# Branch B's first three blocks summed together with K outermost, one gate moved into the mLSTM's last head, and four waits given other orders

## The chip, the core and the metric

The kernel runs on one core of a Trainium2 chip. The metric is device time in microseconds, the median of several runs. A core has five engines that run beside each other: TensorE (PE in the profile: matmuls and transposes; PEld is its loading of weights), VectorE (DVE), ScalarE (ACT), GpSimd (POOL) and SyncE (SP), which here only issues DMAs. SPq and ACTq in a timeline are the DMAs that SP and ScalarE issue. TensorE writes its results into PSUM, eight banks of 128 x 512 fp32.

## The reference

One block of a hybrid layer on x of 1024 positions x 1024 channels, all in fp32. What matters of it:

```
h    = rmsnorm(x, norm_g)
proj = h @ w_in                    # a_q a_k a_v a_o a_z a_g  b_q b_k b_v b_z  g_a g_b
y_a  = rmsnorm(mlstm(conv(a_q), conv(a_k), a_v, forward and backward)) * sigmoid(a_o) * silu(a_z)
y_b  = rmsnorm(diff_attention(rope(b_q), rope(b_k), b_v)) * silu(b_z)
mix  = sigmoid(g_a + gb0) * (y_a @ w_branch_a) + sigmoid(g_b + gb1) * (y_b @ w_branch_b)
out  = rmsnorm(x + mix @ w_out, final_g)
```

The mLSTM has 4 heads of 256, the differential attention 8 heads of 128. The "gates" below are g_a and g_b: 16 blocks of 128 channels.

## The kernel before, in words

**Matmuls.** Every fp32 operand is split in a high and a low part (H, L) that TensorE takes at its fast fp32 rate, and each product is three matmuls: H·H, H·L, L·H. The high part is a cast on ScalarE, the low part a subtraction on VectorE or GpSimd. A projection block (`proj`, L556) is 128 output channels in two halves of 512 positions; a half is 24 matmuls (eight k, three each) into one bank "pj", cut into eight pieces of three matmuls (`PIECES`). There are two pj banks.

**Weights.** `load_w` (L196) loads a block's raw weights by DMA, casts them to wH on ScalarE (L225) and subtracts on GpSimd to wL (L230, or L228 in eight steps while the mLSTM runs). There are three wH/wL pairs and two raw tiles. `run` (L527) walks the list of units, prepares weights up to two blocks ahead where a pair is free, and asks for the raw tile of the one behind.

**Order.** The work is a list of units, each some instructions of TensorE with what follows them on other engines. TensorE executes them in the list's order; the orders of the other engines are made by the framework's scheduler. `Weaver.add` appends units as they come. `Weaver.weave` (L110) merges two lists: it keeps a planned clock from the units' costs, and puts next the unit that can start first, by planned delays (`LAG`) and by how long a bank stays taken (`hold`). If one list is at its end, what is left of the other stands alone.

**Stages.** After the opening and the projections of the mLSTM (to about 510 us) come:

1. Attention, eight heads of eight cycles (`da_cycle`, L1166). Cycle t has S(t), the scores; T, eight transposes of the cycle before's probabilities into the two T banks, which are emptied by the cast pH on ScalarE (L1107) and the subtraction pL on VectorE (L1108); in even cycles PV, 48 matmuls; in odd cycles M, two transposes of the result `att` into a T bank with squares on ScalarE. M(3) of a head falls in cycle 1 of the next one and starts a chain of small operations on GpSimd (L1135 to L1138) that gives rb_y. G(0) and G(1), four transposes of rb_y each, follow in cycles 2 and 4, and after each VectorE writes half of y_b and SP stores it. Each head's cycles (`main`) are woven with the next head's q and k projections, rope included, and the like (`nxt`).
2. The mLSTM (`ml_units`, L1391): per head and t, T transposes the weights W, I multiplies with the states, P is W·v, S the next scores; weigh and state update the states from kw. W is made on GpSimd, ScalarE and VectorE from the gate rows gb, k and v. Two `share` numbers per t say how many gate pieces stand ahead of I and behind S. Nine of the gates lie here; the last head's outputs O and its hm scaling come behind them ("late").
3. Two more gates, 32 pieces: 5 ahead of `late`, 3 behind, 24 woven with eight loads of y_b (`load_y`, L1461: DMA to yraw, four tiles; cast on ScalarE, L1465; subtraction on VectorE, L1466). A gate's end (L976) is a tanh on ScalarE into one tile gt and a store that SP issues (L979).
4. Branch B (`mix_units`, L1473): eight blocks, each half summing all eight y_b in one pj bank before the next half starts; then branch A and the output.

## Time and profile before

| | us |
|---|---|
| median of 3 runs | 1687.43 (1687.06 to 1691.82) |
| the profiled execution | 1685.78 |
| its span, first to last instruction | 1684.0 |
| TensorE busy | 1637.8 |
| VectorE / ScalarE / GpSimd busy | 1023.6 / 766.7 / 669.0 |
| mean granted TensorE clock | 0.993 |

How to read the views. The list of waits has one line for each waiting group and its releaser: us in total, times, the longest. A timeline row is start, duration, engine, line of the kernel, operation, tile written <- tiles read, count, and in brackets the idle time of the engine ahead of it and what ended it. A row of the windows is a stretch, its length, then for PE, PEld, DVE, ACT and POOL the busy time with the count of instructions, then the granted clock of TensorE, the busy share of the DMA engines and GB/s. Matmuls overlap in their pipeline: one is about 0.4 us long, but the next starts about 0.23 us after it.

### The profile page before, as it was taken

How to read it: one execution, taken by the hardware profiler on the slowest of the kernel's cores; microseconds unless marked ns; L12 is line 12 of the kernel's file. 1: busy time of each engine (PE TensorE's matmuls, PEld its weight loads, DVE VectorE, ACT ScalarE, POOL GpSimd, SP SyncE). 2: the span in 40 equal slices, each digit the busy share in tenths (PEclk: the TensorE clock that was granted, in tenths of full speed). 3: DMA queues.
4: the chain of work that ended last, by engine and by line, in shares of the span. 5: the costliest groups of instructions: out<-in, count | busy, mean ns of one | idle time of the engine just before them, and what ended most of it. 6: DMA issues, size and time to landing. Idle time of an engine off the chain costs nothing. (4 is left out here: it accounts for less than half of the span.)

```text
span 1684.0 us, 25335 instructions
## 1 busy us (share of the span) xinstructions
PE 1637.8 (97%) x9335; PEld 1375.7 (82%) x9335; DVE 1023.6 (61%) x1817; ACT 766.7 (46%) x1548; POOL 669.0 (40%) x713
## 2 busy tenths in 40 slices
PE   7999999999999999999999999999999998999998
PEld 6898778878778778888878878888988877888886
DVE  5633787686755776777677686614576764145533
ACT  7433555555434444544454445524566744132221
POOL 5744676766652552624445252132222221222000
PEclk9999999999999999999999999999999999999999
DMA  5434444444442312213132221139876427453222
GB/s 184 146 121 132 124 131 138 123 129 123 126 150 63 88 51 68 72 38 89 45 83 56 63 70 48 54 106 295 258 214 199 145 95 256 149 164 99 75 100 76
DMA packets 189711, 199.76 MB, mean 119 GB/s; under 512 B 11930, under 2 KB 143347, under 8 KB 189587
## 3 DMA queue, kind: packets, MB, share of 16 engines
q1 hardware_dynamic: 188386, 196.03, 38.4%
q10 hardware_dynamic: 1200, 2.11, 0.3%
q8 instruction: 74, 1.21, 0.3%
q14 instruction: 51, 0.41, 0.1%
HBM read 124.60 MB, written 56.72 MB: 108 GB/s over the span
## 5 line engine op out<-in xcount | busy, mean ns | idle before, releaser
L570 PE MATMUL pj<-hH,wH 128*128 128x512 f32 x640 | 261.9, 409 | 1.5 <-ACT f L683 1.5
L570 PE MATMUL pj<-hH,wL 128*128 128x512 f32 x640 | 252.5, 395 | 1.3 <-POOL wL L228 1.3
L570 PE MATMUL pj<-hL,wH 128*128 128x512 f32 x640 | 251.6, 393 | 0.0
L1086 DVE TENSOR_REDUCE nm<-S 128x1 f32<-128x1024 f32 x128 | 150.7, 1219 | 110.7 <-PE S L1083 110.7
L230 POOL TENSOR_TENSOR wL<-raw,wH 128x1024 fp32r<-128x1024 f32 x34 | 85.3, 2509 | 186.5 <-ACT wH L225 184.1
L1107 ACT CAST pH<-T 128x512 fp32r<-128x512 f32 x128 | 68.8, 589 | 169.9 <-PE T L150 169.9
L1088 ACT ACTIVATE e<-S,nm 128x1024 f32<-128x1024 f32 x128 | 142.6, 1129 | 7.4 <-DVE nm L1086 7.4
L570 PEld LDWEIGHTS pj<-hH,wL 128*128 128x128 f32 x640 | 121.0, 189 | 29.5 <-POOL wL L228 3.1
L570 PEld LDWEIGHTS pj<-hH,wH 128*128 128x128 f32 x640 | 121.7, 190 | 20.8 <-ACT f L683 1.8
L570 PEld LDWEIGHTS pj<-hL,wH 128*128 128x128 f32 x640 | 121.2, 189 | 19.5 <-DVE hL L721 0.3
L570 PE MATMUL pj<-sl_yb,wH 128*128 128x512 f32 x384 | 121.2, 396 | 4.5 <-DVE sl_yb L1466 2.9
L1083 PE MATMUL S<-kst,qq 64*128 64x512 f32 x768 | 106.1, 408 | 0.0
L1094 DVE SCALAR_TENSOR_TENSOR e<-e,r,e 128x1024 f32<-128x1024 f32 x64 | 101.5, 1587 | 1.8
L225 ACT CAST wH<-raw 128x1024 fp32r<-128x1024 f32 x48 | 50.6, 1055 | 106.5 <-PE pj L570 85.4
L1083 PEld LDWEIGHTS S<-kst,qq 64*128 64x128 f32 x768 | 67.4, 184 | 29.8 <-issue 9.7
L570 PEld LDWEIGHTS pj<-sl_yb,wH 128*128 128x128 f32 x384 | 73.3, 191 | 21.6 <-DVE sl_yb L1466 3.8
L367 PE MATMUL T<-TH,wH 128*128 128x512 f32 x256 | 87.0, 399 | 1.8 <-ACT u L374 1.8
L367 PE MATMUL T<-TH,wL 128*128 128x512 f32 x256 | 86.1, 397 | 1.1 <-ACT u L374 1.1
L514 DVE SCALAR_TENSOR_TENSOR pj<-cin,cols,pj 128x512 f32<-128x512 f32 x128 | 87.0, 749 | 0.0
L1108 DVE TENSOR_TENSOR pL<-T,pH 128x512 fp32r<-128x512 f32 x128 | 82.0, 682 | 5.9 <-ACT pH L1107 5.9
L215 POOL TENSOR_TENSOR wL<-raw,wH 128x512 fp32r<-128x512 f32 x32 | 51.1, 1609 | 67.7 <-ACT wH L214 62.5
L570 PE MATMUL pj<-sl_yb,wL 128*128 128x512 f32 x192 | 75.7, 394 | 0.0
(398 smaller groups left out, 4425.2 us busy)
## 6 DMA issues: line engine op xcount, KB each, us to landing
raw<-in_w_in_dram SPq DMA_DIRECT2D x84, 512.0 KB, 4.0
kst<-hl SPq DMA_DIRECT2D x64, 128.0 KB, 2.4
qq<-hl SPq DMA_DIRECT2D x64, 128.0 KB, 2.4
x<-in_x_dram SPq DMA_DIRECT2D x8, 512.0 KB, 6.2
avH<-tz SPq DMA_DIRECT2D x16, 256.0 KB, 2.0
cak<-y SPq DMA_DIRECT2D x16, 256.0 KB, 2.8
cakH<-cin SPq DMA_DIRECT2D x16, 256.0 KB, 4.8
cakL<-tz SPq DMA_DIRECT2D x16, 256.0 KB, 4.7
```

The costliest lines, as they stand in the source:

```text
L215: self.p.tensor_tensor(out=vw(wL), in0=src, in1=vw(wHf), op=ALU.subtract)
L225: self.a.copy(wH, raw)
L230: self.p.tensor_tensor(out=wL, in0=raw, in1=wHf, op=ALU.subtract)
L367: self.t.matmul(ps, lhsT=l[:, k, :], rhs=r[:, k, :], start=(first and k == 0 and m == 0), stop=(k == 3 and m == 2), skip_group_check=not f ...
L514: v.scalar_tensor_tensor(out=acc, in0=raw[:, o + x:o + x + 512], scalar=w(x), in1=acc, op0=ALU.mult, op1=ALU.add)
L570: self.t.matmul(ps, lhsT=l[:, k, :], rhs=r, start=(n == 0), stop=(n == 23))
L1083: self.t.matmul(ps[:, o], lhsT=qq[r, x, c], rhs=k[r, y, o], start=(m == 0), stop=(m == 2))
L1086: v.tensor_reduce(out=nm, in_=ps, axis=AX.X, op=ALU.max, negate=True)
L1088: a.activation(out=e, in_=ps, func=AF.Exp, bias=nm[:, 0:1], accum_out=Z[:, j, t:t + 1])
L1094: v.scalar_tensor_tensor(out=e0, in0=e, scalar=r[:, 0:1], in1=e0, op0=ALU.mult, op1=ALU.add)
L1107: a.copy(pH[:, :, s], ps)
L1108: v.tensor_tensor(out=pL[:, :, s], in0=ps, in1=pH[:, :, s].bitcast(F32), op=ALU.subtract)
```

## The change

- Branch B: a new `first_units` computes blocks 0, 1 and 2 together. Six banks (a new pool of T banks in the place of the mLSTM's) hold their two halves each; the outer loop runs over k, so that y_b k is used by all of them before y_b k+1. Block 2 runs two steps behind the others. `mix_units` does blocks 3 to 7 as before.
- Gates: ten instead of nine lie in the mLSTM, in the last head's shares and behind it; 16 pieces are left: 5 ahead of `late`, 3 behind, 4 after the first four loads of y_b and 4 after the others. From there on a gate's stores are issued by ScalarE instead of SP (`late`).
- Attention: G goes from cycles 2 and 4 to 3 and 5. The last unit of each head's list, M(2), becomes the first of the next head's.
- mLSTM: the load of gb for chunk 0 of the first head goes from behind the first loads of k and v to right behind the first of them; eight DMAs that stood ahead of it (a v is two) now stand behind it.

```
+GROUP = 3
...
-            (self.a if self.opening else self.q).dma_start(out=self.tg[seg][i][...], in_=t)
+            (self.a if self.opening or self.late else self.q).dma_start(out=self.tg[seg][i][...], in_=t)
...
-        if prev and t in (2, 4):
-            un.append(prev["G"](t // 2 - 1))
+        if prev and t in (3, 5):
+            un.append(prev["G"]((t - 3) // 2))
...
-        un += x["k"](3) + x["v"](3) + x["k"](2) + x["v"](2) + x["k"](1) + x["v"](1) + hl(x, 0)
+        un += x["k"](3) + x["gb"](0) + x["v"](3) + x["k"](2) + x["v"](2) + x["k"](1) + x["v"](1) + x["HL"](0)
...
-                other, share = gates, ((2, 2), (1, 1), (2, 1), (2, 1), (2, 1), (2, 1), (2, 0), (1, 0))
+                other, share = gates, ((2, 2), (2, 2), (2, 2), (2, 2), (2, 2), (2, 1), (2, 1), (2, 1))
...
+    def first_units(self, st):
+        box = {}
+        def piece(i, half, k):
+            if k == 0:
+                box[i, half] = self.bank("T")
+            ps, (wH, wL), (yH, yL) = box[i, half], self.wt[("w_branch_b", 128 * i)], st["gb", k]
+            c = slice(half * 512, (half + 1) * 512)
+            for m, (l, r) in enumerate(((wH, yH), (wH, yL), (wL, yH))):
+                self.t.matmul(ps, lhsT=l[:, k, :], rhs=r[:, c], start=(k == 0 and m == 0), stop=(k == 7 and m == 2))
+            if k == 7:
...
+                self.v.scalar_tensor_tensor(out=m, in0=box["tg", i][:, c], scalar=1.0, in1=ps, op0=ALU.add, op1=ALU.mult)
+        def gates():
+            for i in range(GROUP):
...
+                self.q.dma_start(out=box["tg", i], in_=self.tg["gb"][i])
+        un = [Unit(0.0, gates)]
+        for step in range(8 + 2):
+            for i in range(GROUP):
+                k = step if i < 2 else step - 2
+                if 0 <= k < 8:
+                    un += [Unit(3 * MM, lambda i=i, half=half, k=k: piece(i, half, k), ...) for half in range(2)]
+        return un
...
-                main = sum((self.da_cycle(cur, prev, t) for t in range(8)), [])
+                main = kept_m + sum((self.da_cycle(cur, prev, t) for t in range(8)), [])
+                main, kept_m = main[:-1], main[-1:]
...
-            w.add(do(lambda: setattr(self, "ml", False)), leave("ps2", "w2"), enter("wy", "wy", side="right"))
+            w.add(do(lambda: setattr(self, "ml", False)), leave("ps2", "w2"), enter("wy", "wy", side="right"), banks("ps3", T=6))
...
-            w.weave(loads, rest[cut:])
...
+            group, passB = self.first_units(st3), self.mix_units("gb", st3, GROUP)
+            w.add(*loads[:4], *[do(lambda i=i: self.load_w(("w_branch_b", 128 * i))) for i in range(2)], *rest[8:12], *loads[4:], *rest[12:])
+            w.add(leave("h"), enter("wr", "wr"), *group)
```

## The prediction

> **What bounds the kernel now.** I read four views in this order: the page, the waits of TensorE, the windows with the granted clock, and the timeline around each long wait.

> ```profile
> span 1684.0 us, 25335 instructions
> ...
> PE 1637.8 (97%) x9335; PEld 1375.7 (82%) x9335; DVE 1023.6 (61%) x1817; ACT 766.7 (46%) x1548; POOL 669.0 (40%) x713
> ```

> TensorE is busy for 1637.8 of 1684.0 us. So it sets the end, and only its 46.2 us of idle time, or time in which its clock is low, can be won without removing matmuls. The change removes none: the 144 matmuls of the three grouped blocks and all their loads exist before and after. So the question is which waits of TensorE go and what comes in their place. The waits of PE, longest in total first (waiting group, releaser, us, times, longest):

> ```profile
> PE T L150 <- POOL rb_y L1138: 3.4, 1, 3.4
> ...
> PE pj L570 <- DVE sl_yb L1466: 2.9, 2, 2.1
> PE T L146 <- ACT kwH L1233: 2.6, 4, 2.0
> ...
> PE T L150 <- DVE pL L1108: 2.0, 1, 2.0
> ...
> PE pj L570 <- ACT sl_yb L1465: 1.6, 2, 1.1
> ```

> Four places hold these: the end of attention head 0 (pL), head 1's second cycle (rb_y), the start of the mLSTM (kwH), and the start of branch B (sl_yb). Around them the windows show the clock (the number ahead of the DMA share and GB/s):

> ```profile
> 576.40:579.50 3.10, 1.08 (x7) 0.92 (x7) 2.75 (x5) 3.10 (x8) 3.10 (x5) 1.00 0.53 147
> 579.50:583.00 3.50, 3.50 (x10) 2.75 (x9) 1.76 (x3) 0.46 (x3) 3.33 (x4) 0.51 0.44 107
> ...
> 608.90:612.30 3.40, 0.35 (x3) 0.35 (x4) 0.87 (x4) 0.68 (x1) 2.99 (x7) 1.00 0.89 202
> 1411.20:1415.80 4.60, 1.72 (x4) 0.67 (x4) 2.70 (x2) 3.09 (x4) 2.32 (x1) 1.00 0.91 298
> 1415.80:1422.60 6.80, 5.63 (x13) 4.46 (x14) 1.80 (x2) 1.04 (x1) 0.03 (x1) 0.50 0.83 279
> ```

> Two of the four places pay twice: after the wait, TensorE runs at half clock for 3.5 us (0.51) and for 6.8 us (0.50). Half of that is lost: 1.7 and 3.4 us.

> **The change part by part.**

> *M(2) goes into the next head's list.* In each attention head the last unit of cycle 7 is M(2), two transposes of `att` into a T bank.

> ```profile
> 575.35 1.09 PE L150 MATMUL T<-ident,e 128*128 128x128 f32 x8
> ...
> 577.72 1.28 DVE L1108 TENSOR_TENSOR pL<-T,pH 128x512 fp32r<-128x512 f32 x2
> ...
> 578.46 0.44 PE L150 MATMUL T<-ident,att 128*128 128x128 f32 x2 [2.02 <-DVE pL L1108]
> 578.65 0.48 PE L570 MATMUL pj<-hH,wH 128*128 128x512 f32 x1
> ...
> 587.25 1.65 PE L1083 MATMUL S<-kst,qq 64*128 64x512 f32 x12
> ...
> 595.43 1.65 PE L1083 MATMUL S<-kst,qq 64*128 64x512 f32 x12
> ```

> At the end of head 0 nothing is left to put between: the eight transposes fill both T banks, and M(2) waits 2.02 us until VectorE has emptied the first. Right behind it stand projection matmuls of the next head that wait for nothing. Once M(2) is in the next list, the planner puts these first; they are the cover (8.6 us of them, from 578.65 to the next scores at 587.25), and nobody waits close behind M(2). The wait goes, 2.0 us, and I take the low clock after it to go too, 1.7 us: **3.7 us**. If the cover were gone, the 2.0 us would be back.

> *G from cycles 2 and 4 to 3 and 5.*

> ```profile
> 608.77 1.68 POOL L166 TENSOR_TENSOR rb_y<-rb_v,mhalf 128x8 f32<-128x8 f32 x1
> ...
> 611.66 0.23 POOL L1138 TENSOR_SCALAR rb_y<-rb_y 128x8 f32<-128x8 f32 x1
> ...
> 611.95 0.65 PE L150 MATMUL T<-ident,rb_y 128*128 128x128 f32 x4 [3.45 <-POOL rb_y L1138]
> ```

> G(0) of head 0 stood in cycle 2 and waited 3.45 us for GpSimd's short chain, which had been queued behind the rope work. One cycle more is 8.2 us (from 587.25 to 595.43), twice what was missing. So **3.4 us**. What waits for G: its store of y_b leaves SP a cycle later, and nobody reads that before branch B; its zg buffer comes free a cycle later, and the planner holds the gate z of the next head, which stands at the end of the list of cycles, 6 us behind it. That is still ahead of its place. What the move may cost is the new neighbour: cycles 3 and 5 now hold G and M, both wanting one of two T banks behind the transposes.

> ```profile
> PE T L1119 <- DVE pL L1108: 1.4, 4, 0.5
> ```

> That row, from the waits again, is the nearest price: four PV units wait 0.35 us each. The bounds are those four gone (-1.4) and 16 G units at 0.35 (+5.6); I take four more such waits, **-1.4 us**, since M in odd cycles waits nowhere but in head 0.

> *The load gb(0) goes ahead of v(3).*

> ```profile
> 1138.34 0.60 SPq L1205 DMA_DIRECT2D gb<-gg  x1
> ...
> 1145.96 1.24 POOL L1288 TENSOR_SCALAR_AFFINE_SELECT W<-gb 128x128 f32<-128x128 f32 x4 [10.16 <-DMA gb<-gg]
> 1146.28 0.40 ACT L1290 ACTIVATE W<-W,gc_negM 128x128 f32<-128x128 f32 x1 [4.01 <-POOL W L1288]
> ...
> 1146.59 0.46 ACT L1233 ACTIVATE kwH<-T,gc_ws 128x256 fp32r<-128x256 f32 x1
> ```

> This is the 2.0 us wait for kwH. ScalarE stood 4.01 us at the exponential of W, which needs gb, which landed 7.6 us after its issue; kwH was queued behind it. gb(0) moves past eight loads of SP, 4.8 us at 0.60 each, and the exponential is then free before kwH's turn: **2.0 us**. Each of those loads starts one issue later (0.60 us). Bounds: 2.0 down to nothing, if ScalarE's order moves the exponential forward too and the wait only changes its kwH.

> *One gate more in the last head.* From 1330 us on, TensorE's waits are these:

> ```profile
> 1336.39 0.50 PE L146 MATMUL PO<-vH,WH 128*128 128x256 f32 x2 [0.88 <-ACT WH L1350]
> ...
> 1355.64 0.33 PE L150 MATMUL T<-ident,W 128*128 128x128 f32 x1 [0.47 <-ACT W L1335]
> ...
> 1373.73 0.44 PE L150 MATMUL T<-ident,W 128*128 128x128 f32 x2 [0.41 <-DVE W L1337]
> ...
> 1377.03 0.71 PE L150 MATMUL T<-ident,W 128*128 128x128 f32 x2 [0.72 <-ACT W L1335]
> ...
> 1384.48 1.97 PE L150 MATMUL T<-ident,hm 128*128 128x128 f32 x8 [0.54 <-ACT hm L1368]
> 1386.95 1.22 PE L150 MATMUL T<-ident,hm 128*128 128x128 f32 x8 [0.50 <-ACT hm L1368]
> ```

> A piece of a gate is three matmuls, 0.68 us (0.226 each, next part). The new shares put one more piece ahead of the wait at 1336.4 (0.68 of 0.88 covered) and behind the scores of cycle 3 (the 0.47 at 1355.6), cycle 6 (0.41) and cycle 7 (0.68 of 0.72). Cycle 5 gets none. Ahead of the hm transposes 11 pieces stand instead of 7, 2.7 us more, so their 1.0 goes. Sum **3.2 us**; bounds 2 and 4.5.

> *Branch B's start.* The gate stores go to ScalarE's queue, 11 gate pieces instead of 27 stand ahead of branch B, and its first 48 units run with K outermost.

> ```profile
> 1440.00:1600.00 160.00, 160.00 (x708) 132.48 (x707) 65.61 (x85) 35.16 (x49) 27.99 (x12) 1.00 0.34 110
> ```

> ```profile
> 1386.83 2.58 SPq L1381 DMA_DIRECT2D ya<-gA  x4
> ...
> 1391.02 0.32 SPq L979 DMA_DIRECT2D tga<-gt  x1
> ...
> 1391.44 1.83 SPq L1463 DMA_DIRECT2D yraw<-yb  x4
> ...
> 1397.10 1.05 ACT L1465 CAST sl_yb<-yraw 128x1024 fp32r<-128x1024 f32 x1 [6.10 <-DMA yraw<-yb]
> ...
> 1398.18 1.23 DVE L1466 TENSOR_TENSOR sl_yb<-yraw,sl_yb 128x1024 fp32r<-128x1024 f32 x1 [9.12 <-ACT sl_yb L1465]
> ...
> 1399.81 2.41 POOL L230 TENSOR_TENSOR wL<-raw,wH 128x1024 fp32r<-128x1024 f32 x1 [14.29 <-ACT wH L225]
> ...
> 1400.66 6.05 DVE L1466 TENSOR_TENSOR sl_yb<-yraw,sl_yb 128x1024 fp32r<-128x1024 f32 x4 [1.25 <-ACT sl_yb L1465]
> ```

> The pace of matmuls where nothing waits is 160 us / 708 = 0.226 us. Before, 81 gate matmuls follow the hm transposes, whose last starts at about 1387.9, up to 1406.2; then block 0 walks through all eight y within 24 matmuls, 5.4 us, per half, faster than they arrive: 4.5 us of waits (2.9 and 1.6 above) and 3.4 of low clock, 7.9 together. After, 33 gate matmuls end at 1395.4 on the same scale. SP no longer holds the y loads behind the gate store, which waited for its tanh, so they issue when the four ya stores are out, 1389.4; with the same 5.7 us the first lands at 1395.1. Cast (1.05) and subtraction (1.23) make it ready at 1397.4: TensorE waits 1.8 us after its first matmul. Then eleven matmuls, 2.5 us. The second y comes 6.2 us after the first one landed, as now: ScalarE puts a tanh and a weight cast between, and the subtraction of y runs beside GpSimd's weight split (2.41) and takes 2.6 instead of 1.23 (6.05 less three at 1.14). That is 1401.3, so 1.2 us more. From there K needs a new y every 2.7 us, later 4.1 (18 matmuls), and y 2 to 7 come faster. So 3.0 us of waits stay, in two pieces too short to lower the clock by the rows above: 7.9 - 3.0 = **4.9 us**. The third block's weights are split by 1400.2 and wanted at about 1404; that lead of two steps is the cover, and without it some 4 us come back. Two stores on ScalarE cost 0.32 us each by SP's row, ahead of y casts at worst; I leave that in the range. Bounds: all 7.9, or nothing.

> **The sum.** 3.7 + 3.4 - 1.4 + 2.0 + 3.2 + 4.9 = 15.8 us. The profiled execution took 1685.78 us, 1.8 more than its span; less 15.8 that is 1670.0. The median of the runs shown, 1687.43, lies 1.65 above it, so I say **1671.6 us**.

> **The rivals.**

> *The low clock stays.* The half-clock stretches follow waits of 2.02 us and, at 1411 to 1416, of 2.9 us in several pieces, but the longest wait, 3.45 us, had a clock of 1.00 in its window (608.9 to 612.3). If the stretches are not caused by these waits, 5.1 us stay: 1676.7. [...] Chance 0.08.

> *The wait at branch B only moves.* If the y loads start no earlier, because something other than the gate store holds them, the first is ready at 1399.4, 4.0 us after the group starts, then 1.2, then a low clock again: all 4.9 us are lost, 1676.5. For it: the ya stores are still in flight at 1391. Against it: the y loads issue at the very end of the gate store. Chance 0.14.

> *The gb load does nothing* (ScalarE takes the exponential earlier, and the wait falls on the first kwH): 1673.6. Chance 0.06.

> *Slower: T banks.* If G finds no bank behind the transposes, each G costs what M(2) cost in head 0, 2.0 us; fourteen G units in running heads make 28 us: 1699.6. It decides against the change from 15.8 / 14 = 1.13 us per G. Against it: M stands in the same place in all heads and waits once only. Chance 0.05.

> **How the numbers follow.** The forecast has 0.67. A measurement of this kernel can tell about 0.3%, 5.1 us, from no change. All cases but the T banks end over 5.1 us faster by themselves; two misses together, or an edge of the range, give the middle: faster 0.87, same 0.07, slower 0.06. Low end: the branch B stall and the last head's waits all gone, no new small waits: some 6.6 us better, 1665. High end: the gb load and branch B both give nothing and some new waits come: 1680.

> **What would show it.** In the changed profile: no wait on rb_y L1138 over 1 us and none of M on pL; 1.00 clock near 580 us; no long ACT gap at L1290 at the mLSTM's start; W waits of 1 to 1.5 us in the last head, none for hm; the group's first matmuls waiting about 2 us, then 1 us, for sl_yb, with full clock behind. Wrong would be: many waits of T on pL in cycles 3 and 5, a wait of the third block on wL, or half clock after the group's start.

## The result, and the profile after

The changed kernel takes 1673.07 us (median of 5 runs, 1672.69 to 1675.12) against 1687.06 us for the kernel before beside it (5 runs, 1683.0 to 1691.82): a ratio of 0.9919, 95% interval 0.9898 to 0.9939, so 0.6 to 1.0% faster. The forecast was 1671.6 us. The profiled execution is the one of 1673.07 us. The medians differ by 14.0 us and the two profiled executions by 12.7, where 15.8 were forecast. The next sections show that the total came out near the forecast partly by luck: two misses of 7.9 us together, against two unforeseen gains of 4.35.

The page of the changed kernel, and its waits of TensorE (waiting group, releaser, us, times, longest). Lines of this kernel stand 2 higher than before in the parts at issue.

```profile
span 1671.2 us, 25342 instructions
...
PE 1631.7 (98%) x9335; PEld 1373.4 (82%) x9335; DVE 1013.5 (61%) x1817; ACT 770.1 (46%) x1548; POOL 664.0 (40%) x720
```

```profile
PE T L1485 <- ACT sl_yb L1467: 3.3, 1, 3.3
PE T L148 <- ACT kwH L1235: 3.3, 4, 2.7
...
PE T L1121 <- DVE pL L1110: 1.9, 5, 0.7
...
PE PO L148 <- ACT WH L1352: 0.8, 3, 0.3
...
PE T L152 <- ACT W L1337: 0.7, 1, 0.7
PE T L152 <- DVE W L1339: 0.7, 2, 0.4
...
PE T L1485 <- DVE sl_yb L1468: 0.5, 1, 0.5
```

Gone are the 3.4 us on rb_y, the 2.0 us on pL at the end of head 0, and the waits for hm; the W waits of the last head fell from 2.8 to 1.4 us. But kwH still makes TensorE wait, longer than before (2.7 us at once instead of 2.0), and branch B still starts with a wait, 3.3 us in one piece.

The windows show what came behind the last two: each was followed by a half clock (the figure ahead of the DMA share).

```profile
1128.90:1132.30 3.40, 0.70 (x4) 0.31 (x2) 0.35 (x1) 2.18 (x6) 1.24 (x4) 1.00 1.04 354
1132.30:1135.70 3.40, 3.40 (x15) 2.95 (x15) 1.30 (x4) 0.67 (x3) 0.00 (x0) 0.50 1.06 370
1395.10:1398.50 3.40, 0.29 (x2) 0.00 (x0) 0.00 (x0) 0.92 (x1) 0.00 (x0) 1.00 1.01 380
1398.50:1405.30 6.80, 6.16 (x14) 4.49 (x15) 5.40 (x4) 5.42 (x7) 2.39 (x1) 0.50 0.84 304
```

To see where the time went I compare starts of the same work in both traces: the first scores of attention, the last G, the first mLSTM scores of heads 0 and 3 (SS), and the end of the 144 matmuls of branch B's first three blocks.

| stage | before, us | after, us | gain | forecast |
|---|---|---|---|---|
| start to first scores | 518.1 | 516.5 | 1.65 | 0 |
| first scores to last G | 610.3 | 601.9 | 8.4 | 5.7 |
| last G to first SS | 27.7 | 29.9 | -2.2 | 2.0 |
| mLSTM heads 0 to 2 | 170.7 | 170.8 | -0.1 | 0 |
| last head, then 144 matmuls of B | 120.7 | 116.05 | 4.6 | 8.1 |
| from there to the last matmul | 228.7 | 228.7 | 0 | 0 |
| sum | | | 12.4 | 15.8 |

Behind the last matmul lie 0.4 us more, in the final stores: the spans differ by 12.8. Each stage holds the same matmuls in both kernels, but for 48 of the gate that moved within the fifth row.

Within that row I take the time that TensorE lost in the last head: each distance between two matmuls, less the median distance of such a pair in the whole trace. It is 10.8 us before and 7.3 after. So 3.45 us were won in that head, and 1.2 us in branch B.

The start of the mLSTM in the changed kernel (start, us, engine, operation, in brackets the idle time before and what ended it):

```profile
1122.17 0.68 ACT L980 ACTIVATE gt<-pj,gbh 128x512 f32<-128x512 f32 x1
...
1122.87 0.32 SPq L981 DMA_DIRECT2D tgb<-gt  x1
...
1123.24 0.43 SPq L1207 DMA_DIRECT2D gb<-gg  x1
...
1129.79 1.24 POOL L1290 TENSOR_SCALAR_AFFINE_SELECT W<-gb 128x128 f32<-128x128 f32 x4 [4.05 <-DMA gb<-gg]
...
1130.12 0.86 ACT L1292 ACTIVATE W<-W,gc_negM 128x128 f32<-128x128 f32 x2 [7.27 <-POOL W L1290]
...
1131.46 0.46 ACT L1235 ACTIVATE kwH<-T,gc_ws 128x256 fp32r<-128x256 f32 x1
...
1132.02 0.36 PE L148 MATMUL T<-vH,kwH 128*128 128x258 f32 x1 [2.70 <-ACT kwH L1235]
```

SyncE reached gb only at 1123.24, behind a gate's store that waits for its tanh; gb landed 6.5 us later; and ScalarE, which now has the exponential of W ahead of the first kwH, stood 7.27 us there. The start of branch B:

```profile
1388.20 0.38 SPq L194 DMA_DIRECT2D raw<-in_w_branch_b_dram  x1
...
1388.68 2.46 SPq L1383 DMA_DIRECT2D ya<-gA  x4
...
1390.76 0.33 ACTq L981 DMA_DIRECT2D tga<-gt  x1
...
1391.23 9.00 SPq L1465 DMA_DIRECT2D yraw<-yb  x5
...
1397.58 1.04 ACT L1467 CAST sl_yb<-yraw 128x1024 fp32r<-128x1024 f32 x1 [6.85 <-DMA yraw<-yb]
...
1398.68 0.80 PE L1485 MATMUL T<-sl_yb,wH 128*128 128x512 f32 x1 [3.29 <-ACT sl_yb L1467]
```

The gate's store is off SyncE, and the y loads still start at 1391.23: raw weights of 512 KB, held until GpSimd had split the weights before them (to 1388.2), and four ya stores stand ahead of them. The DMA engines are then full (1.01 in the window above, 380 GB/s).

### The profile page after: what moved, and what is told of

It is laid out like the page before. It is cut to its first block, busy times and chain, and to the rows that moved or that the text cites. A ratio compares the mean times of both kernels' runs of the same rounds, so it can differ in the third digit from the quotient of the medians.

```text
span 1671.2 us, 25342 instructions
## 1 busy us (share of the span) xinstructions
PE 1631.7 (98%) x9335; PEld 1373.4 (82%) x9335; DVE 1013.5 (61%) x1817; ACT 770.1 (46%) x1548; POOL 664.0 (40%) x720
## 3 DMA queue, kind: packets, MB, share of 16 engines
q8 instruction: 74, 1.21, 0.3%
## 5 line engine op out<-in xcount | busy, mean ns | idle before, releaser
L572 PEld LDWEIGHTS pj<-hH,wL 128*128 128x128 f32 x640 | 120.1, 188 | 29.9 <-POOL wL L230 3.7
L572 PEld LDWEIGHTS pj<-hL,wH 128*128 128x128 f32 x640 | 120.7, 189 | 19.4 <-DVE hL L723 0.6
L1096 DVE SCALAR_TENSOR_TENSOR e<-e,r,e 128x1024 f32<-128x1024 f32 x64 | 93.4, 1459 | 1.8
L572 PE MATMUL pj<-sl_yb,wH 128*128 128x512 f32 x288 | 88.6, 389 | 0.0
L217 POOL TENSOR_TENSOR wL<-raw,wH 128x512 fp32r<-128x512 f32 x32 | 47.1, 1486 | 77.1 <-ACT wH L216 71.9
L230 POOL TENSOR_TENSOR wL<-raw,wH 128x128 fp32r<-128x128 f32 x120 | 59.4, 530 | 42.1 <-ACT wH L227 37.7
L152 PEld LDWEIGHTS T<-ident,e 128*128 128x128 f32 x512 | 54.9, 141 | 23.8 <-issue 23.7
```

The costliest lines, as they stand in the source:

```text
L152: self.t.transpose(out, in_, self.ident[0:k, 0:k])
L230: self.p.tensor_tensor(out=wL[:, k], in0=raw[:, k], in1=wHf[:, k], op=ALU.subtract)
L572: self.t.matmul(ps, lhsT=l[:, k, :], rhs=r, start=(n == 0), stop=(n == 23))
L1096: v.scalar_tensor_tensor(out=e0, in0=e, scalar=r[:, 0:1], in1=e0, op0=ALU.mult, op1=ALU.add)
```

## The experiments

Twelve kernels, in four groups; each group ran on one chip with the kernel before beside it, and a ratio is to that kernel there (after: 0.9919, 0.9898 to 0.9939). The median of the kernel before was 1683.7, 1685.4, 1682.7 and 1683.8 us in the groups, so absolute times are not compared across them; the stages of the profiles are. "Stage M" is from the last G to the first SS (before 27.7, after 29.9 us), "stage B" from the first SS of the last head to the end of the 144 matmuls (120.7 and 116.05), "stretch h" from the last transpose of hm to that end (after: 47.4).

**The attention edits alone**, on the kernel before.

```
+        if prev and t in (3, 5):
+            un.append(prev["G"]((t - 3) // 2))
...
+                main = kept_m + sum((self.da_cycle(cur, prev, t) for t in range(8)), [])
+                main, kept_m = main[:-1], main[-1:]
```

> The kernel before with the two attention edits alone: G in cycles 3 and 5, M(2) in the next head's list. Theory 1 (the prediction's terms 3.7 + 3.4 - 1.4): 5.7 us faster than before. Theory 2 (the changed kernel's marks in this stage, without its new small waits): 7.1 to 8.3 us faster. Rival (T banks): slower. In all: from the first scores to the last G the stretch is 8 us shorter than before by theory 2, with no wait of 1 us on pL or rb_y and no half clock near 580 us.

Ratio 0.9948 (0.9933 to 0.9963), about 8.8 us. From the first scores to the last G 601.2 us, 9.1 less than before; no half clock near 580. Its waits of T for pL:

```profile
PE T L1119 <- DVE pL L1108: 1.0, 2, 0.7
```

There are fewer of these waits than before (two instead of four), and none at M. But their sum, 1.4 us in the kernel before, lies between 0.8 and 2.4 us in the thirteen kernels with this order of attention, so what G beside M costs in bank waits is not told apart from nothing. The stage gains 7.8 to 9.4 us in these thirteen. Theory 2 holds, with a little more than its upper figure. The rival falls.

**gb(0) back at its old place**, in the changed kernel.

```
-        un += x["k"](3) + x["gb"](0) + x["v"](3) + ... + x["v"](1) + x["HL"](0)
+        un += x["k"](3) + x["v"](3) + ... + x["v"](1) + hl(x, 0)
```

> The changed kernel with the load gb(0) back behind v(1), where it was before. Theory 1 (the prediction's): the early load was worth 2.0 us, so this kernel takes 1675.1 us against 1673.1, with the longest wait of TensorE at the start of the mLSTM going up. Theory 2 (the trace of the changed kernel): the early load won nothing, because it only moved the wait from the second kwH (2.0 us) to the first (2.7 us) and brought a half-clock stretch of 3.4 us (1.7 us lost); then the wait is 2.0 us at the second kwH again, no half clock near 1132 us, and the kernel is 0.6 to 2.4 us faster, 1670.7 to 1672.5.

Ratio 0.9919 (0.9904 to 0.9934). The longest wait for kwH is 2.1 us, at the second kwH as before; stage M is 29.0 us, 0.9 less than in the changed kernel. Six other kernels here share that kernel's code in stage M; the seven lie between 29.4 and 31.1 us, so 29.0 is little outside their spread. The early load won nothing: theory 1 is wrong. Theory 2 is right on the wait but not on the clock: a half clock of 3.4 us came all the same, from 1135.7. The kernel before has the same 2.0 us wait and no half clock (27.7 us); why is told in the last section.

**Gate stores of the end of attention on ScalarE's queue**, in the changed kernel, so that SyncE reaches gb(0) sooner.

```
+            w.add(do(lambda: setattr(self, "late", True)))
             w.weave(end[:-2], fill(2))
...
+            w.add(do(lambda: setattr(self, "late", False)))
             ml, late = self.ml_units(...)
```

> The changed kernel with the gate stores of the end of attention (three gates of branch B) on ScalarE's queue, so that SyncE reaches gb(0) without waiting for the last tanh. Theory 1 (SyncE, held by that store, issues gb(0) too late): gb is issued about 3 us earlier than 1123.2, W is ready before the first kwH, the 2.7 us wait on kwH and the half clock of 3.4 us at 1132 us (1.7 us lost) go, and the time is 3 to 4.4 us under the changed kernel's (profiled 1668.7 to 1670.1). Rival (the transfer is what is late, 6.5 us, or kwH waits for something else): gb lands where it did and the time stays within 0.7 us of 1673.1.

Ratio 0.9942 (0.9927 to 0.9957), stage M 29.4 us: no gain. Counted from the last G, gb was issued 2.0 us later instead of 4.9, and GpSimd's W started 9.6 us later instead of 11.5, but then this stood ahead of kwH:

```profile
1130.63 1.56 ACT L1292 ACTIVATE W<-W,gc_negM 128x128 f32<-128x128 f32 x4 [5.39 <-POOL W L1290]
...
1132.88 0.69 ACT L980 ACTIVATE gt<-pj,gbh 128x512 f32<-128x512 f32 x1 [0.69 <-DMA tgb<-gt]
...
1133.47 0.47 ACT L1235 ACTIVATE kwH<-T,gc_ws 128x256 fp32r<-128x256 f32 x1
...
1134.04 0.40 PE L148 MATMUL T<-vH,kwH 128*128 128x258 f32 x1 [2.31 <-issue]
```

gb took 7.5 us to land, and all four exponentials, where it was two, came ahead of kwH. Behind them the next gate's tanh waited 0.69 us more, until the store of the one before it had landed, at 1132.80, 7.5 us after its issue: there is one gt tile. SyncE's order was not the only cause; the rival is nearer.

**gb(0) later instead**, behind the loads of HL(0).

```
-        un += x["k"](3) + x["gb"](0) + x["v"](3) + ... + x["v"](1) + x["HL"](0)
+        un += x["k"](3) + x["v"](3) + ... + x["v"](1) + x["HL"](0) + x["gb"](0)
```

> The changed kernel with gb(0) not earlier but later than before: behind the loads of HL(0), which puts ScalarE's exponential of W behind both kwH of the second weigh. Theory 1 (it is the place of that exponential in ScalarE's order, against a transfer of 6.5 to 7.6 us, that makes TensorE wait; where gb is issued only chooses which kwH pays): no wait for kwH over 1 us at the start of the mLSTM, and from the last G to the first scores of the mLSTM 27.7 us (the kernel before) less about 2, so 25.2 to 26.5 us, or 1.7 more if a half clock falls there; the time 2 to 4 us under the changed kernel's. Rival (the wait only falls on the next kwH again): a wait of about 2 us on a later kwH, and 28 us or more.

Ratio 0.9924 (0.9908 to 0.9941). One wait of 1.0 us is left, stage M is 28.85 us with a half clock of 3.4 us in it (from 1144.0); the same edit gives 27.2 us without one, in the kernel with both edits below. A half clock of 3.4 us costs 1.7 (the granted clock is 0.50 in it), so this edit is worth about 0.5 us against the 27.7 of the kernel before. Theory 1 is right that ScalarE's order sets the wait, but it gave less than it said, for the same single tile stood in the way again:

```profile
1140.74 0.69 ACT L980 ACTIVATE gt<-pj,gbh 128x512 f32<-128x512 f32 x1 [3.20 <-DMA tgb<-gt]
...
1142.38 0.36 PE L148 MATMUL T<-vH,kwH 128*128 128x258 f32 x1 [1.03 <-POOL W L1290]
```

The page names GpSimd's W as the releaser of TensorE; the kwH that it needs came late because of the 3.20 us at this tanh.

**Gate stores back on SyncE**, in the changed kernel.

```
-            (self.a if self.opening or self.late else self.q).dma_start(...)
+            (self.a if self.opening else self.q).dma_start(...)
```

> The changed kernel with the last gates' stores on SyncE's queue, as before the change. Theory 1 (the prediction's): the store that waits for its tanh held the y loads, so the first y is issued 2 us later than in the changed kernel (1391.2) and the group's first wait grows from 3.3 to about 5 us: 1675 us. Theory 2: the raw weights and the four ya stores hold SyncE until 1391.1 anyway, so the store costs one issue, 0.3 to 0.4 us: the first wait is 3.3 to 3.7 us and the time 1673.1 to 1673.5.

Ratio 0.9925 (0.9909 to 0.9942); the group's wait is 3.7 us and stage B 116.3 us, 0.3 longer. Theory 2: this edit of the change is worth one issue at most, since stage B lies between 116.0 and 116.5 us in the four kernels that have the changed kernel's code there.

**Without the gate's move, and without K outermost.** Two kernels: the last head keeps its old shares and 27 gate pieces stand ahead of the group, 24 of them behind the loads of y0 to y3; or all eight blocks run block by block, with the gate moved.

```
-                other, share = gates, ((2, 2), (2, 2), (2, 2), (2, 2), (2, 2), (2, 1), (2, 1), (2, 1))
+                other, share = gates, ((2, 2), (1, 1), (2, 1), (2, 1), (2, 1), (2, 1), (2, 0), (1, 0))
...
-            cut = len(rest) - 2 * self.PIECES
+            cut = len(rest) - 4 * self.PIECES
```

> The changed kernel without the gate's move: the last head keeps its old shares, and 27 instead of 11 gate pieces stand between it and the group; the first three blocks still run with K outermost. Theory 1 (the prediction: the move gives 3.2 us in the last head, and the group waits about the same): 3.2 us slower than the changed kernel. Theory 2 (the 10.8 us of gate work were the cover of the y loads, and the group's stall of 3.8 us with the half clock of 6.8 us behind it, 3.4 us lost, is the price of moving them): the group starts with y0 to y2 there and waits under 1 us at full clock, so 7.1 - 3.3 = 3.8 us faster than the changed kernel (profiled about 1669.3).

```
-            group, passB = self.first_units(st3), self.mix_units("gb", st3, GROUP)
+            passB = self.mix_units("gb", st3)
```

> The changed kernel with all eight blocks of branch B block by block, as before (no K outermost), the gate still moved. Theory 1 (K outermost spreads the need for y): block 0 walks through eight y in 5.4 us per half right at 1395 us while they land until about 1412, so the waits at the start of branch B come to 10 us or more and the kernel is 6 us or more slower than the changed kernel. Rival (the transfers hold the pace in either order, and the half clock hides part of the wait): within 2 us of it.

Ratios 0.9931 (0.9914 to 0.9947) and 0.9985 (0.9974 to 0.9995). Stage B in the four kernels:

| stage B, us | gate ahead of B | gate in the last head |
|---|---|---|
| block by block | 120.7 | 124.1 |
| K outermost | 113.8 | 116.05 |

The corner of 120.7 is the kernel before. There the y loads are also woven otherwise among the gates' pieces and SyncE issues the stores, so the first row and the first column hold these differences too. Read across: moving the gate costs 3.4 or 2.2 us, though the last head alone gains 3.45. Read down: K outermost gives 6.8 or 8.0 us. With the gate ahead of the group, no wait at branch B is left at all. The gate's pieces were the cover of the y loads; theory 2 is right in kind, with 2.2 instead of 3.8 us. The whole kernel was no faster than the changed one, since it had half clocks in other places (81.9 and 1136.6 us, and 1382.4 inside stage B). Without K outermost theory 1 holds, at 8 us.

**y0 to y3 issued by GpSimd**, whose queue is empty after 1388.2, in the changed kernel.

```
-        self.q.dma_start(out=raw, in_=src[i])
+        (self.p if src is self.yb and i < 4 else self.q).dma_start(out=raw, in_=src[i])
```

> The changed kernel with the first four y loads of branch B issued by GpSimd, which has nothing queued after its weight split at 1388.2. Theory 1 (SyncE's order holds the loads: raw weights, then four ya stores): the first y is issued at about 1388.3 instead of 1391.2, lands about 2.9 us earlier, and the group's first wait falls from 3.3 to under 1 us; with the half clock of 6.8 us behind it gone as well the kernel takes 1667 to 1670 us, with the half clock left 1670 to 1671. Theory 2 (the transfers ahead of y, raw and ya, fill the DMA engines, which were 1.00 busy from 1390 on): y lands within 0.7 us of where it did (1397.6), and the time stays within 1 us of 1673.1.

Ratio 0.9934 (0.9919 to 0.9949). y0 was issued at 1387.3 and landed at 1393.4, 4.2 us earlier (3.4 against the last transpose of hm), and the group's first wait fell to 0.8 us. But waits of 1.5 and 2.1 us followed, for the high and then the low part of y1, the half clock moved to 1401.2, and stage B is 116.8 us: nothing won. In the windows the DMA engines stay full from 1391 to 1409 at 354 to 417 GB/s; three gate loads of 512 KB had moved ahead of y4. Neither theory is right alone.

**The group's gate loads behind y3 on GpSimd's queue as well.**

```
-                self.q.dma_start(out=box["tg", i], in_=self.tg["gb"][i])
+                self.p.dma_start(out=box["tg", i], in_=self.tg["gb"][i])
```

> The run with the first four y loads on GpSimd again, and the three 512 KB gate loads of the group behind them on the same queue, so that they no longer run ahead of y. Theory 1 (the DMA engines' rate of 0.4 MB per us is the limit, and what counts is how many bytes stand ahead of each y): y0 lands at about 1393, y1 to y3 by 1398, the group's waits come to 1 us instead of 4.4, the half clock of 6.8 us behind them is gone, and the stretch from the last hm transpose to the end of the group is 5 to 7 us shorter than in the changed kernel (47.4 us): profiled 1666 to 1668. Theory 2 (y is bound by what each load takes from its issue on, or by ScalarE and VectorE): the waits only move to y1 to y3 again, and the time stays within 1.5 us of 1673.1.

Ratio 0.9939 (0.9925 to 0.9954); the waits are again 0.8, 1.5 and 2.1 us, stretch h 48.1 us. Theory 1 falls in this form: y1 had landed at 1397.1 and was cast at 1400.04. What held it:

```profile
1398.52 0.69 ACT L980 ACTIVATE gt<-pj,gbh 128x512 f32<-128x512 f32 x1 [3.00 <-DMA tga<-gt]
...
1399.11 1.04 ACT L227 CAST wH<-raw 128x1024 fp32r<-128x1024 f32 x1
...
1400.04 2.94 ACT L1467 CAST sl_yb<-yraw 128x1024 fp32r<-128x1024 f32 x3
1400.28 2.35 POOL L232 TENSOR_TENSOR wL<-raw,wH 128x1024 fp32r<-128x1024 f32 x1 [7.83 <-ACT wH L227]
1401.12 3.73 DVE L1468 TENSOR_TENSOR sl_yb<-yraw,sl_yb 128x1024 fp32r<-128x1024 f32 x2 [4.34 <-ACT sl_yb L1467]
1401.14 0.49 PE L1485 MATMUL T<-sl_yb,wH 128*128 128x512 f32 x1 [1.53 <-ACT sl_yb L1467]
...
1403.78 0.80 PE L1485 MATMUL T<-sl_yb,wH 128*128 128x512 f32 x1 [2.14 <-DVE sl_yb L1468]
```

The last half gate's tanh needs the one gt tile, whose store was issued at 1391.16, while the DMA engines, by the windows of the run before, were full (1.03 from 1391 to 1394); ScalarE stood 3.00 us, with the weight cast and y1's cast behind. That is the first wait, of 1.53 us. The second, of 2.14 us, has another cause: the subtraction that makes y1's low part, the first of the two in the row, ran beside GpSimd's weight split and took 2.6 us, where the subtractions of y that overlap no split took 1.2.

**A tile of its own for that tanh**, on top of the last kernel.

```
-            t = self.wpool.tile([128, 512], F32, name="gt", tag="gt")
+            t = self.slot("mb", F32)[:, 0:512] if self.late and half else self.wpool.tile([128, 512], F32, name="gt", tag="gt")
```

> The run with y0 to y3 and the group's gate loads on GpSimd, and besides the last gate half's tanh gets a tile of its own instead of the single one it shared. In the run before this one ScalarE stood 3.0 us at that tanh, for the store of the half before it to land, with y1's cast, already landed at 1397.1, queued behind it until 1400.0. Theory 1 (that queueing on ScalarE makes the two waits of 1.5 and 2.1 us and the half clock behind them): the tanh runs right after y0's cast, y1 is cast 2.5 to 3 us earlier, the waits for y1 and y2 come to under 1.5 us together and the half clock of 6.8 us (3.4 us lost) shortens or goes: 3 to 6 us less than that run from the last hm transpose to the end of the group (48.1 us there). Theory 2 (the transfers alone set the pace): those two waits stay within 0.7 us, and the stretch within 1.5 us.

Ratio 0.9924 (0.9908 to 0.9940).

```profile
1396.72 0.69 ACT L980 ACTIVATE sl_mb<-pj,gbh 128x512 f32<-128x512 f32 x1 [0.45 <-PE pj L572]
...
1398.24 1.05 ACT L1467 CAST sl_yb<-yraw 128x1024 fp32r<-128x1024 f32 x1
```

```profile
PE T L1485 <- POOL wL L232: 2.3, 1, 2.3
...
PE T L1485 <- DVE sl_yb L1468: 0.7, 1, 0.7
```

The tanh no longer waits for a store, y1 is cast 0.2 us after it landed, both waits for y1 are gone (the 0.7 us left is for y0) and so is the half clock; stretch h is 44.2 us, 4.0 less. Theory 1 holds for the cast. It does not have all of the gain: y1's subtraction took 1.2 us again, because GpSimd's split no longer ran beside it but started only at 1406.5. That split is what is late next. GpSimd stood 13 us (12.99 in the kernel of both, below) at the first of the gate loads that the edit before had put on its queue ahead of the split; without the new tile these loads had gone out from 1390.9 on.

**Both** (gb behind HL(0), and the branch B edits), and **with GpSimd's split ahead of the gate loads**, the only further edit:

```
-        un = [Unit(0.0, gates)]
+        un = []
         for step in range(8 + 2):
+            if step == 4:
+                un.append(Unit(0.0, gates))
```

> The two runs before this one together: y0 to y3 and the group's gate loads on GpSimd, a tile of its own for the last tanh, gb(0) behind HL(0). If both theories hold their gains add, as they lie in stages 250 us apart: 5 to 9 us under the changed kernel's 1673.1, and faster than both kernels. If only one does, its own gain.

> The run of both edits, with one more: GpSimd takes the weight split of the third block ahead of the group's three gate loads. In the run before, GpSimd stood 13 us at the first of these loads, and the split (2.4 us) came so late that TensorE waited 2.2 us for it, with a half clock of 3.4 us behind (1.5 us lost). Theory 1 (that order makes this wait): the wait for wL is gone, with it the half clock, and the stretch from the last hm transpose to the end of the group falls from 45.7 to 41.5 to 42.5 us; 3 to 4 us less in all, 1664 against 1667.2 profiled. Rival (y4 to y7 come no earlier, so the group waits for y at the next step instead): the stretch stays above 44.5 us.

The first: ratio 0.9909 (0.9894 to 0.9923), profiled 1667.2 us, stage M 27.2, stretch h 45.7 us: the wL wait of 2.2 us brought a half clock this time. The second: ratio 0.9902 (0.9879 to 0.9924), median 1666.05 us of six runs (1664.81 to 1668.89); no wait for wL, full clock through the group, stretch h 43.0 us, 0.5 more than expected, for TensorE now waits 1.2 us for the low part of y1, whose subtraction runs beside the split again:

```profile
PE T L1485 <- DVE sl_yb L1468: 2.0, 2, 1.2
```

```profile
1397.53 2.39 POOL L232 TENSOR_TENSOR wL<-raw,wH 128x1024 fp32r<-128x1024 f32 x1 [6.70 <-ACT wH L227]
...
1398.37 3.77 DVE L1468 TENSOR_TENSOR sl_yb<-yraw,sl_yb 128x1024 fp32r<-128x1024 f32 x2 [1.62 <-ACT sl_yb L1467]
...
1401.06 0.50 PE L1485 MATMUL T<-sl_yb,wH 128*128 128x512 f32 x1 [1.24 <-DVE sl_yb L1468]
```

Its profiled execution took 1668.9 us instead of the expected 1664: it has half clocks at 82.0 and 1143.6 us that the one of the first had not.

The second is 4.5 us better than the changed kernel in stretch h and 0.9 in stage M (29.0 us; a half clock falls into it in both). Both beat the kernel before; that the second beats the changed one is shown by stretch h, not by the ratios, whose intervals overlap. Where GpSimd stood:

```profile
1403.70 1.10 POOL L1495 DMA_DIRECT2D tgl<-tgb  x2 [3.78 <-DMA tga<-sl_mb]
```

The gate loads wait for the store of that tanh's tile. That their memory hangs together I infer from this line; no run tried it.

## Why the prediction was right, and where not

- **M(2), G.** Right in cause and size, though the two edits were not run apart: no wait for rb_y or for pL at M, and full clock at 580. The two waits and the half clock were put at 7.1 us; by the scores of head 1's fifth cycle the changed kernel is 6.7 us ahead, counted from the first scores.
- **"What the move may cost is the new neighbour", -1.4 us.** Not borne out. The PV waits of T for pL were 1.4 us before, are 1.9 in the changed kernel and lie between 0.8 and 2.4 with this order of attention, so no run shows such a cost. The stage gave 8.4 us here and 9.1 with the attention edits alone, instead of 5.7. TensorE's idle time in it fell from 7.9 to 2.7 us and the half clock gave 1.7; the last 1.5 us of the 8.4 show as no wait, and their cause stays open. The rival of the T banks fell.
- **"The exponential is then free before kwH's turn", 2.0 us.** This step failed. The load did move forward by 5.0 us, as forecast (issued 4.9 instead of 9.95 us after the last G). But the bound named what came of it: ScalarE's order moved the exponential forward too, and gb, behind a store that waits for its tanh, still took 6.5 us. The rival had this at no gain; stage M lost 2.2 us, as the wait grew to 2.7 and a half clock, 1.7 of them, fell behind it. No place of the load was free: early, it stops the first kwH, at the old place the second, and later the single gt tile takes over with 1.0 us.
- **The gate in the last head, 3.2 us.** Right in that head: 3.45. But the prediction put at nothing what the gate's pieces had covered at branch B; the table above has that at 2.2 to 3.4 us more than the gain.
- **Branch B, 4.9 us.** Measured 1.2. The step that failed is "SP no longer holds the y loads behind the gate store": raw weights and the ya stores hold them (1391.2 instead of 1389.4), the store is worth 0.3 us. The rival there, "the wait at branch B only moves", came nearest, though its reason was not known. Issued earlier, y0 landed 4.2 us earlier, but then ScalarE's one gt tile and a subtraction of 2.6 us beside GpSimd's split made y1 late. How much the full DMA engines add is read from the windows only; no run tried it apart. The waits came as 3.3 and 0.5 us with 6.8 us of half clock, where 1.8 and 1.2 without one were forecast.
- **The low clock.** The case that it stays had 0.08; it went at 580, stayed at branch B and came up at the start of the mLSTM. In these runs the length of a wait alone did not tell: 2.1 us (gb(0) at its old place) and 2.7 us (the changed kernel) were followed by a half clock, 3.45 us (the kernel before) was not.

So 15.8 us were forecast and 12.4 measured up to the last matmul, of which 1.65 belong to no edit. The sum was near and its terms were not, which is luck in part: attention gave 2.7 more, the start of the mLSTM 4.2 less, branch B 3.7 less.

## What to carry to other kernels

Work moved into a hole fills it, but ask first what it covered where it stood: here 16 gate pieces won 3.45 us in the last head and cost more at branch B. When a load is moved forward, look at what the engine that consumes it has queued behind the consumer (here kwH, behind an exponential at which ScalarE stood 7.27 us), and at every tile with a single buffer on that engine: a store that had to land before the buffer could be written again held ScalarE for 3.0 and 3.2 us here. Before two engines are given work at the same time, look what each takes beside the other (2.6 instead of 1.2 us here, for VectorE's subtraction beside GpSimd's weight split). Judge edits of 2 us by stages of the profile, and look for a half clock in the stage too, since one of 3.4 us made the time jump by 1.7 us here.

## What the runs showed of the hardware

```profile
77.80:81.20 3.40, 1.65 (x15) 1.44 (x13) 0.91 (x1) 1.05 (x1) 3.32 (x2) 1.00 0.72 197
576.20:579.60 3.40, 1.38 (x9) 1.02 (x8) 3.02 (x6) 3.40 (x8) 3.40 (x5) 1.00 0.51 143
579.60:583.00 3.40, 3.40 (x9) 2.65 (x9) 1.69 (x2) 0.37 (x2) 3.23 (x4) 0.50 0.42 101
606.90:610.30 3.40, 1.60 (x8) 0.99 (x6) 2.87 (x7) 2.68 (x5) 3.40 (x4) 1.00 0.56 128
610.30:613.70 3.40, 1.75 (x15) 1.75 (x16) 1.06 (x2) 0.00 (x0) 2.99 (x7) 1.00 0.78 180
613.70:617.10 3.40, 3.40 (x24) 3.08 (x22) 1.64 (x1) 0.37 (x1) 0.56 (x1) 1.00 0.50 143
```

The wait of 2.0 us fell into one window (1.38 of 3.40 busy), and the next ran at half clock; the wait of 3.45 us was cut in two by the grid (1.60 and 1.75 busy), and the clock stayed at 1.00. Over the fourteen profiled executions, of the windows between 10 and 1650 us at full clock in which TensorE was idle for 53% or more, 22 of 22 were followed by a half clock; from 35 to 53%, 12 of 34; from 25 to 35%, 1 of 35; below that, none of 6589. In the traces of the kernel before and the changed kernel alone these are 4 of 4, 2 of 6, none of 7 and none of 933. These edges were set after seeing the windows, and in the middle the share alone does not settle it: 1.65 of 3.40 busy was followed by a half clock at 77.8 us, 1.60 was not at 606.9.

That accounts for the 1.65 us that no edit made. At 80 us both kernels have the same wait for wL of 1.8 us; in the kernel before the window that holds it was busy for 1.65 us, and the next ran at half clock; in the changed kernel it fell so:

```profile
77.60:81.00 3.40, 2.07 (x18) 1.86 (x16) 1.50 (x1) 1.63 (x3) 3.40 (x2) 1.00 0.45 122
81.00:84.40 3.40, 2.90 (x24) 2.90 (x25) 0.00 (x0) 0.03 (x1) 3.26 (x5) 1.00 0.62 187
```

Of the twelve experiments seven had that half clock and five had not, with the same code there. The same holds at the start of the mLSTM, where the wait for kwH of 2.0 us in the kernel before brought no half clock and that of 2.1 us with gb(0) at its old place did. Such a wait thus cost itself here or 1.7 us more, by where it lay on the grid: the first was cut in two (2.31 and 2.49 of 3.40 busy), the second fell into one window (1.31 of 3.40 busy). In the last kernel most of the spread between its runs is lost clock: the fastest, 1664.8 us, had a mean granted clock of 0.999 and the slowest, 1668.9, one of 0.997, which is about 3.3 of the 4.1 us (an estimate, 0.002 of the span).

VectorE's subtractions of y at branch B, eight in each of the fourteen executions, took 1.21 to 1.23 us where GpSimd's weight split did not run at the same time (95 of them) and 2.59 to 3.37 us where it did (17).
